# Where 76 transposes of a hybrid encoder layer are made: TensorE with an identity, or DMA transposes of two 16-bit planes

## The chip, the cores and the metric

One Trainium2 chip, one of its cores. The metric is the device time of one execution in microseconds. Lower is better. The kernel before has a median of 1718.32 us over 3 runs (1717.17 to 1718.71).

## The reference

One layer of a streaming encoder with 320 positions (256 of a new stream, 64 of a running stream that also sees 256 cached positions), d = 2048, 8 attention heads of 128, 8 gating groups of 128. Cut to what matters here:

```python
proj = rmsnorm(x) @ w_in                       # q, k, v, u, vs, gates
z = (q @ k.T) * 128**-0.5                      # per head
w = where(mask, exp(log_sigmoid(z) + log_rest), 0)   # stick-breaking weights
a = w @ v                                      # contraction over key positions
vs = rmsnorm(gelu(vs)); s = w_s @ vs + b_s     # gating: contraction over positions
bb = gelu(u) * s
merged = g_a * (a @ w_branch_a) + g_b * (bb @ w_branch_b)
h = x + merged @ w_out
y = rmsnorm(h + (silu(gu[:ff]) * gu[ff:]) @ w_down)
```

All inputs and outputs are float32. The outputs are y, the new k and v rows and the normalised vs rows of the 64 running positions.

## The kernel before, in words

Activations lie with features on the 128 partitions and the 320 positions (T) along the free dimension. Every projection is made by `block` (line 87), 128 output features at a time: the weights come in half blocks of 8 x 128 rows (512 KB) through `weights` (line 68). SP issues the load into one of 3 `raw` buffers, ScalarE rounds it to `wh` (line 75), VectorE takes the rest `wl = raw - wh` (line 76), 4 buffers each, and TensorE makes three float32r matmuls of 320 columns for each of the 8 pieces (lines 83, 84 and 85: wh with the high and the low part of the activation, wl with the high part). One half block is 24 matmuls. After each half block `tick` (line 62) counts one up and runs the functions that `at` (line 58) has put down for that tick: all work of attention and of the spatial gate is placed between half blocks in this way. A scheduler then orders each engine's instructions by what it reckons to be ready; only what goes through `keep_in_program_order` keeps its place behind its engine's previous instruction.

Attention goes by pairs of heads. `head_out` (line 421) scales a finished q, k or v block, issues the store of k and v from GpSimd, and for v copies the 64 running positions into the tile `vo` (line 431). `attend` (line 438) puts down four steps for a pair: `att_scores` 2 ticks later (scores on TensorE, lines 342 to 345, then the chain of abs, exp, ln, scan and exp on ScalarE and VectorE, lines 349 to 374, that ends in the weights `z[0]`, `z[1]` and `wown`), `att_rows` at 4 ticks (load of the cached v rows), `att_turn` at 10 ticks, `att_out` at 14 ticks. `att_turn` (line 376) makes 14 transposes of 128 x 128 float32 on TensorE against `ident`: 4 of v (line 383), 1 of `vo` (384), 6 of the prompt's weights (387), 2 of the weights on the cache (389) and 1 of `wown` (390), into 4 PSUM banks, and evacuates them with three ScalarE copies (393, 396, 397) and two VectorE copies (394, 395) to `wt` and `av`. `att_out` (line 399) multiplies from these and splits the result into the activations `aT`. A pair comes every 12 ticks; there are 4.

The spatial gate goes by pairs of groups, 4 of them: `sgu_gain` (line 477) scales vs and stores the running rows, `sgu_turn` (487) makes 5 transposes (lines 490, 491) and evacuates them with two ScalarE copies (494, 495), `sgu_mix` (499) multiplies by the masked spatial weights (503, 505) and makes `bT`. `sgu_both` (518) runs the mix of one pair and the turn of the next in one tick, every 4 ticks of the 16 that the u blocks take.

Of the kernel before, what the change touches and what calls it, by code (L numbers as in the profile page):

```python
# [8 lines left out]
F32 = mybir.dt.float32  # L9
# [4 lines left out]
P = 128  # L14
TP = 256
TS = 64
T = TP + TS
D = 2048
KD = D // P
H = 8  # L20
# [13 lines left out]
def stream_step(ctx: ExitStack, tc: tile.TileContext, xT, w_in, w_a, w_b, w_out, w_gu, w_down,  # L34
                gains, ws_t, bs, ck_t, cv, y_t, k_t, v_t, sv_t):
    nc = tc.nc
# [65 lines left out]
    def pair(name):  # L102
        return big.tile([P, 2 * T], F32, tag="D", bufs=8, name=name)
# [36 lines left out]
    ident = const.tile([P, P], F32, name="ident")  # L140
# [142 lines left out]
    attn = {}  # L283
    att_ctx = ExitStack()
    apool = att_ctx.enter_context(tc.tile_pool(name="attn", bufs=1))
# [21 lines left out]
    Z, KT = 384, T + PAST  # L307
# [13 lines left out]
    def att_new(p):  # L321
        attn[p] = {"q": apool.tile([P, 2, T], F32, tag="q", bufs=2, name="q"),
                   "k": apool.tile([P, 2, KT], F32, tag="k", bufs=2, name="k"),
                   "v": apool.tile([P, 2, T], F32, tag="v", bufs=2, name="v"),
                   "vo": apool.tile([P, P], F32, tag="vo", name="vo")}

    def att_keys(p):
        tc.keep_in_program_order(nc.sync.dma_start(
# [44 lines left out]
        for r in ROWS:  # L373
            nc.scalar.activation(out=wown[r, r], in_=z[1][r, Z:], func=AF.Exp)

    def att_turn(p):

        s = attn[p]
        z, v = s["z"], s["v"]
        ba, bb, bs_, bv = aux(), aux(), aux(), aux()  # L380
        cols = lambda t, i: t[:, i * P : (i + 1) * P]
        for i in range(4):
            nc.tensor.transpose(cols(bv, i), v[:, i // 2, i % 2 * P : (i % 2 + 1) * P], ident)  # L383
        nc.tensor.transpose(cols(ba, 3), s["vo"], ident)
        for j, b in enumerate((ba, bb)):
            for i in range(3):
                nc.tensor.transpose(cols(b, i), cols(z[j], i), ident)  # L387
        for i in range(2):
            nc.tensor.transpose(cols(bs_, i), cols(z[0], 3 + i), ident)
        nc.tensor.transpose(cols(bs_, 2), wown, ident)  # L390
        wt = s["wt"] = apool.tile([P, 3 * Z], F32, tag="wt", name="wt")
        av = s["av"] = apool.tile([P, 5 * P], F32, tag="av", name="av")
        nc.scalar.copy(out=av[:, 0 : 4 * P], in_=bv)
        nc.vector.tensor_copy(wt[:, 0:Z], ba[:, 0:Z])
        nc.vector.tensor_copy(av[:, 4 * P :], ba[:, Z:])
        nc.scalar.copy(out=wt[:, Z : 2 * Z], in_=bb[:, 0:Z])
        nc.scalar.copy(out=wt[:, 2 * Z :], in_=bs_[:, 0:Z])

    def att_out(p):
        s = attn.pop(p)  # L400
        wt, av, cvt = s["wt"], s["av"], s["cv"]
        po = aux1(), aux()
        mm = lambda out, a, b, first, last: nc.tensor.matmul(out, a, b, start=first, stop=last, skip_group_check=True)  # L403

        mm(po[0][:, TP : TP + P], av[:, 4 * P :], wt[:, 2 * Z + 2 * P :], True, False)
        for j, r in enumerate(ROWS):
            for i in range(2):
                lo = 2 * Z + i * P + j * TS
                mm(po[0][:, TP + j * TS : TP + (j + 1) * TS], cvt[:, i, j, :], wt[:, lo : lo + TS], False, i == 1)
        for j in range(2):  # L410
            mm(po[j][:, 0:TP], av[:, 2 * j * P : (2 * j + 1) * P], wt[:, j * Z : j * Z + TP], True, False)
            mm(po[j][:, P:TP], av[:, (2 * j + 1) * P : (2 * j + 2) * P], wt[:, j * Z + TP : (j + 1) * Z], False, True)
# [8 lines left out]
    def head_out(name, ps, h):  # L421
        s = attn[h // 2]
        o = s[name][:, h % 2, 0:T]
        if name == "q":
            nc.vector.scalar_tensor_tensor(out=o, in0=ps, scalar=QSCALE, in1=got["rx"],
                                           op0=ALU.mult, op1=ALU.mult)
        else:
            nc.vector.tensor_tensor(out=o, in0=ps, in1=got["rx"], op=ALU.mult)
            nc.gpsimd.dma_start(out=(k_t if name == "k" else v_t)[h], in_=o)
        if name == "v":  # L430
            nc.gpsimd.tensor_copy(s["vo"][:, ROWS[h % 2]], o[:, TP:T])

    def first_out():
        for name, b in (("q", 0), ("k", 1), ("v", 2)):
# [33 lines left out]

    us, _ = halves(H, "us")
    bT: dict[int, tuple] = {}  # L470
    vown, vnat = {}, {}

    def sgu_norm():
        got["rv"] = rms("rv", [sq.total], H * P)
        sgu_gain(0)

    def sgu_gain(p):

        own = vown[p] = apool.tile([P, 2, T], F32, tag="q", bufs=2, name="vown")[:, 0, 0:P]
        for j in range(2):  # L480
            g = 2 * p + j
            for out, r in ((vs[g][:, 0:TP], slice(0, TP)), (own[:, j * TS : (j + 1) * TS], slice(TP, T))):
                nc.vector.scalar_tensor_tensor(out=out, in0=vs[g][:, r], scalar=g_sgu[:, g : g + 1],
                                               in1=got["rv"][:, r], op0=ALU.mult, op1=ALU.mult)
            nc.gpsimd.dma_start(out=sv_t[g], in_=own[:, j * TS : (j + 1) * TS])

    def sgu_turn(p):
        pt, po = aux(), aux()
        for i in range(4):
            nc.tensor.transpose(pt[:, i * P : (i + 1) * P], vs[2 * p + i // 2][:, i % 2 * P : (i % 2 + 1) * P], ident)  # L490
        nc.tensor.transpose(po[:, 0:P], vown.pop(p), ident)
        t = apool.tile([P, 5 * P], F32, tag="av", name="vsn") if p % 2 else apool.tile([P, 3 * Z], F32, tag="wt", name="vsn")
        vn = vnat[p] = t[:, 0 : 5 * P].rearrange("p (i d) -> p i d", i=5)
        nc.scalar.copy(out=vn[:, 0:4].rearrange("p i d -> p (i d)"), in_=pt)
        nc.scalar.copy(out=vn[:, 4], in_=po[:, 0:P])
        if p + 1 < H // 2:
            sgu_gain(p + 1)
# [20 lines left out]
    def sgu_both(p):  # L518
        if p:
            sgu_mix(p - 1)  # L520
        if p < H // 2:
            sgu_turn(p)
# [14 lines left out]
    for m in range(KD):  # L537
        gate = []
        for i in range(2):
            ps = block(w_in[5 * H + i * KD + m], xs)  # L540
            t = t320("ev")
# [8 lines left out]
        t = t320("mg", 1)  # L550
# [5 lines left out]
        lo = mpool.tile([P, T], F32R, tag="C", bufs=32, name="ml")  # L556
# [72 lines left out]
    ms, r = (const.tile([P, 3], F32, name=f"col{i}") for i in range(2))  # L629
# [9 lines left out]
    for n in (1, 1, 2, 2, 2, 2, 2, 2, 1, 1):  # L639
        y = ypair[done // 2].rearrange("p (c t) -> p c t", c=2)[:, done % 2 : done % 2 + n, :]  # L640
# [57 lines left out]
```

## Time and profile before

| | |
|---|---|
| median of 3 runs | 1718.32 us |
| profiled execution, its time | 1716.78 us |
| its span, first to last instruction | 1715.0 us |
| mean granted TensorE clock | 0.998 |
| attention of the first pair to the last gate mix | about 60 to 327 us of the span |
| VectorE, ScalarE, GpSimd busy over the span | 861.9, 658.8, 46.1 us |
| DMA engines' mean rate | 154 GB/s |

The profiled execution is 1.78 us longer than its span (what lies outside the first and the last instruction), and 1.54 us below the median. In the profile's rows, PE is TensorE's matmul, DVE VectorE, ACT ScalarE, POOL GpSimd, SPq the queue of SP that issues loads. A timeline row gives start, duration, engine, line, operation, output and inputs, how many were merged, and in brackets the idle time before it with what ended it. A row of waits gives total, number of times and longest, in us. A row of DMA issues ends with the KB of one and the median us from issue to landing. A row of groups ends with busy us, mean ns of one, and the engine's idle time before.

### The profile page before, as it was taken

The numbers are of one execution on the slowest core, as the hardware profiler recorded it, in microseconds if no ns is written. First come the engines' busy times: TensorE is split into PE (matmuls) and PEld (weight loads), VectorE is DVE, ScalarE is ACT, GpSimd is POOL, SyncE is SP. The second block draws the span as 40 slices with busy tenths as digits, with TensorE's granted clock in tenths as the row PEclk, the third lists the DMA queues.
The fourth block names the chain that finished last, engine by engine and source line by source line (L and its number), as shares of the span: only waits on it lengthen the run. The fifth ranks groups of instructions, "written<-read, shape, count | busy, mean of one in ns | idle before, by whom it ended". The sixth has DMA issues, their size and how long they took to land.

```text
span 1715.0 us, 27450 instructions
## 1 busy us (share of the span) xinstructions
PE 1702.2 (99%) x11616; PEld 1696.7 (99%) x11616; DVE 861.9 (50%) x1097; ACT 658.8 (38%) x819; POOL 46.1 (3%) x73
## 2 busy tenths in 40 slices
PE   9999999999999999999999999999999999999997
PEld 9999999999999999999999999999999999999997
DVE  7655446544444445555444444444444444444454
ACT  6454454433333333444333332233333323333332
POOL 0100011000000000110000000000000000000000
PEclk9999999999999999999999999999999999999999
DMA  7554444444444445554444445444444444444453
GB/s 260 162 193 143 144 154 145 139 148 148 149 153 152 148 152 165 174 171 149 150 148 148 150 152 153 148 148 148 152 151 152 148 148 150 151 153 149 130 150 114
DMA packets 80331, 263.32 MB, mean 154 GB/s; under 512 B 9008, under 2 KB 15408, under 8 KB 80208
## 3 DMA queue, kind: packets, MB, share of 16 engines
q1 hardware_dynamic: 78704, 258.25, 46.6%
q0 software_dynamic: 1088, 3.02, 0.5%
q8 instruction: 91, 1.49, 0.3%
q10 hardware_dynamic: 416, 0.31, 0.1%
q14 instruction: 32, 0.26, 0.0%
HBM read 256.03 MB, written 5.51 MB: 152 GB/s over the span
## 4 chain that ended last, share of the span: by engine, by line
issue 54%; PE 45%; DVE 0%; DMA 0%; ACT 0%; POOL 0%; POOLq 0%; ACTq 0%; DVEq 0%
PE acc L83 13%; PE acc L84 13%; PE acc L85 13%; PE aux L219 2%; PE acc L219 1%; PE aux L403 1%; DVE h L637 0%; DMA raw<-w_in 0%; PE aux L505 0%; PE aux L343 0%; PE aux L345 0%; PE aux L387 0%; PE aux L342 0%; PE aux L490 0%; PE aux L383 0%
## 5 line engine op out<-in xcount | busy, mean ns | idle before, releaser
L75 ACT CAST wh<-raw 128x1024 fp32r<-128x1024 f32 x468 | 484.5, 1036 | 988.0 <-PE acc L84 796.3
L76 DVE TENSOR_TENSOR wl<-raw,wh 128x1024 fp32r<-128x1024 f32 x468 | 564.2, 1206 | 506.4 <-ACT wh L75 503.9
L83 PE MATMUL acc<-A,wh 128*128 128x320 f32 x2464 | 763.1, 310 | 0.0
L85 PE MATMUL acc<-A,wl 128*128 128x320 f32 x2464 | 761.5, 309 | 0.0
L84 PE MATMUL acc<-A,wh 128*128 128x320 f32 x2464 | 761.4, 309 | 0.0
L83 PEld LDWEIGHTS acc<-A,wh 128*128 128x128 f32 x2464 | 462.6, 188 | 2.1 <-issue 2.0
L84 PEld LDWEIGHTS acc<-A,wh 128*128 128x128 f32 x2464 | 462.6, 188 | 0.2
L85 PEld LDWEIGHTS acc<-A,wl 128*128 128x128 f32 x2464 | 462.6, 188 | 0.0
L85 PE MATMUL acc<-B,wl 128*128 128x320 f32 x960 | 296.6, 309 | 0.0
L83 PE MATMUL acc<-B,wh 128*128 128x320 f32 x960 | 296.6, 309 | 0.0
L84 PE MATMUL acc<-B,wh 128*128 128x320 f32 x960 | 296.6, 309 | 0.0
L83 PEld LDWEIGHTS acc<-B,wh 128*128 128x128 f32 x960 | 180.2, 188 | 0.0
L84 PEld LDWEIGHTS acc<-B,wh 128*128 128x128 f32 x960 | 180.2, 188 | 0.0
L85 PEld LDWEIGHTS acc<-B,wl 128*128 128x128 f32 x960 | 180.2, 188 | 0.0
L83 PE MATMUL acc<-mh,wh 128*128 128x320 f32 x256 | 79.1, 309 | 0.0
L84 PE MATMUL acc<-ml,wh 128*128 128x320 f32 x256 | 79.1, 309 | 0.0
L85 PE MATMUL acc<-mh,wl 128*128 128x320 f32 x256 | 79.1, 309 | 0.0
L597 DVE TENSOR_TENSOR bb<-acc,rh 128x320 f32<-128x320 f32 x44 | 21.6, 491 | 57.8 <-PE acc L85 57.8
L594 DVE TENSOR_TENSOR ev<-acc,rh 128x320 f32<-128x320 f32 x44 | 21.6, 491 | 56.4 <-PE acc L85 56.3
L83 PEld LDWEIGHTS acc<-mh,wh 128*128 128x128 f32 x256 | 48.0, 188 | 0.0
L84 PEld LDWEIGHTS acc<-ml,wh 128*128 128x128 f32 x256 | 48.0, 188 | 0.0
L85 PEld LDWEIGHTS acc<-mh,wl 128*128 128x128 f32 x256 | 48.0, 188 | 0.0
(173 smaller groups left out, 696.2 us busy)
## 6 DMA issues: line engine op xcount, KB each, us to landing
raw<-w_gu SPq DMA_DIRECT2D x176, 512.0 KB, 3.5
raw<-w_in SPq DMA_DIRECT2D x141, 512.0 KB, 3.6
raw<-w_down SPq DMA_DIRECT2D x80, 512.0 KB, 3.5
raw<-w_out SPq DMA_DIRECT2D x32, 512.0 KB, 3.6
raw<-w_a SPq DMA_DIRECT2D x16, 512.0 KB, 3.5
raw<-w_b SPq DMA_DIRECT2D x16, 512.0 KB, 3.5
raw<-w_down SPq DMA_DIRECT2D x16, 256.0 KB, 2.7
xr<-xT SPq DMA_DIRECT2D x16, 160.0 KB, 2.6
```

Source lines behind the costliest of these rows:

```text
L75: nc.scalar.copy(out=wh[:, : n * P], in_=raw[:, : n * P])
L76: nc.vector.tensor_tensor(out=wl[:, : n * P], in0=raw[:, : n * P], in1=wh[:, : n * P].bitcast(F32), op=ALU.subtract)
L83: nc.tensor.matmul(ps[:, :T], a, x[0], start=first, stop=False)
L84: nc.tensor.matmul(ps[:, :T], a, x[1], start=False, stop=False)
L85: nc.tensor.matmul(ps[:, :T], b, x[0], start=False, stop=last)
L219: nc.tensor.matmul(first[b][h][:, :T], w[:, (h * n + j) * P : (h * n + j + 1) * P], xs[c + j][i], start=not last and c + j + i == 0, stop= ...
L403: mm = lambda out, a, b, first, last: nc.tensor.matmul(out, a, b, start=first, stop=last, skip_group_check=True)
L594: nc.vector.tensor_tensor(out=t, in0=pg, in1=got["rh"], op=ALU.mult)
L597: nc.vector.tensor_tensor(out=u, in0=pu, in1=got["rh"], op=ALU.mult)
```

## The change

The 76 transposes leave TensorE. In their place GpSimd splits the float32 source into two planes of 16 bits that stand one after the other in a tile (`apart`), SP issues one DMA transpose of 8 or 10 blocks of 128 x 128 16-bit values for the whole tile (`turn`), and VectorE copies the turned planes back into the float32 layout (`together`). One pair of heads has three such tiles: v with its running rows (`vp`, 10 blocks), the weights of `z[0]` (`wp0`, 10) and those of `z[1]` with `wown` (`wp1`, 8). One pair of gating groups has one (`vsp`, 10). That makes 16 DMA transposes, 16 VectorE copies and 40 GpSimd copies. The PSUM evacuations of the transposes go, and so do the `vo` copies.

```diff
+    def planes(name, n):
+        return pair(name)[:, 0:n].bitcast(U16).rearrange("p (w n) -> p n w", w=2)
+    def apart(to, src):
+        nc.gpsimd.tensor_copy(to, src.bitcast(U16).rearrange("p (n w) -> p n w", w=2))
+    def turn(src):
+        n = src.shape[1]
+        to = planes("turned", n)
+        flat = lambda t: t.rearrange("p n w -> p w n").rearrange("p w n -> p (w n)")
+        tc.keep_in_program_order(nc.sync.dma_start(
+            out=flat(to).rearrange("p (b r) -> p b r", r=P), in_=flat(src), transpose=True))
+        return to
+    def together(to, src):
+        nc.vector.tensor_copy(to.bitcast(U16).rearrange("p (n w) -> p w n", w=2), src.rearrange("p n w -> p w n"))
...
+        y = s["wp"] = planes("wp0", 5 * P), planes("wp1", 4 * P)
+        apart(y[0], z[0])
+        apart(y[1][:, 0:Z], z[1][:, 0:Z])
+        apart(y[1][:, Z:], wown)
...
-        for i in range(4):
-            nc.tensor.transpose(cols(bv, i), v[:, i // 2, i % 2 * P : (i % 2 + 1) * P], ident)
...
-        nc.vector.tensor_copy(wt[:, 0:Z], ba[:, 0:Z])
+        s[what] = [turn(t) for t in ((s["vp"],) if what == "vt" else s["wp"])]
+    def att_join(p, what):
...
+            together(av, t[0])
...
+            together(wt[:, 0 : 5 * P], t[0])
+            together(wt[:, 5 * P :], t[1])
...
         at(now + 2, att_scores, p)
-        at(now + 4, att_rows, p)
-        at(now + 10, att_turn, p)
-        at(now + 14, att_out, p)
+        at(now + 6, att_turn, p, "vt")
+        at(now + 8, att_rows, p)
+        at(now + 8, att_join, p, "vt")
+        at(now + 12, att_turn, p, "wt")
+        at(now + 14, att_join, p, "wt")
+        at(now + 16, att_out, p)
...
-    for p in range(H // 2 + 1):
-        at(base + 4 * p + 2 + (p == 0), sgu_both, p)
+    for p, mix in enumerate((9, 11, 14, 18)):
+        at(base + 1 + 3 * p, sgu_gain, p)
+        at(base + 6 + 3 * p, sgu_turn, p)
+        at(base + (8, 10, 13, 16)[p], sgu_join, p)
+        at(base + mix, sgu_mix, p)
```

The order of instructions moves as follows. On TensorE, in the middle of the half blocks behind the first pair's scores (wh and wl are a half block's weights, A an activation, `aux` a PSUM bank), before:

```order
L85 MATMUL acc_997<-A_496,wl_1032 128x320
L383 MATMUL aux_1062<-ident_79,v_623 128x128 x4
L384 MATMUL aux_1059<-ident_79,vo_624 128x128
L387 MATMUL aux_1059<-ident_79,z0_775 128x128 x3
L387 MATMUL aux_1060<-ident_79,z1_776 128x128 x3
L389 MATMUL aux_1061<-ident_79,z0_775 128x128 x2
L390 MATMUL aux_1061<-ident_79,wown_617 128x128
L83 MATMUL acc_1091<-A_154,wh_1094 128x320
```

and at the same place of the changed kernel:

```order
L85 MATMUL acc_1009<-A_496,wl_1044 128x320
L83 MATMUL acc_1078<-A_154,wh_1081 128x320
L84 MATMUL acc_1078<-A_155,wh_1081 128x320
L85 MATMUL acc_1078<-A_154,wl_1082 128x320
L83 MATMUL acc_1078<-A_162,wh_1081 128x320
```

The 14 transposes are gone and one half block follows the other. In the queue of SP, from the cached keys of the second pair on (`raw` is a half block of weights), before:

```order
L328 DMA k<-ck_t 128x2x256
L70 DMA raw<-w_in 128x1024 [waits DMAHW3_49,DVE_49]
L70 DMA raw<-w_in 128x1024 [waits DMAHW4_49,DMAHW0_49,DVE_49]
L70 DMA raw<-w_in 128x1024 [waits DMAHW5_49,DVE_49]
L292 DMA wst<-ws_t 128x1024
L70 DMA raw<-w_in 128x1024 [waits DMAHW7_49,DVE_49]
```

and now:

```order
L348 DMA k<-ck_t 128x2x256
L70 DMA raw<-w_in 128x1024 [waits DMAHW2_49,DVE_49]
L70 DMA raw<-w_in 128x1024 [waits DMAHW3_49,DVE_49]
L340 DMA_TRANSPOSE turned<-vp 128x10x128 [waits Pool_49]
L70 DMA raw<-w_in 128x1024 [waits DMAHW5_49,DVE_49]
L340 DMA_TRANSPOSE turned<-wp_806 128x10x128 [waits Pool_49]
L340 DMA_TRANSPOSE turned<-wp_807 128x8x128 [waits DMAHW4_49,Activation_49,Pool_49]
L292 DMA wst<-ws_t 128x1024
L70 DMA raw<-w_in 128x1024 [waits DMAHW7_49,DMAHW6_49,DVE_49]
```

Three DMA transposes now stand between loads of weights, and each waits for GpSimd. On VectorE, behind the last step of the first pair's score chain (line 370 before, 390 now), before:

```order
L370 TENSOR_TENSOR z_775<-z_775,e 128x640
L76 TENSOR_TENSOR wl<-raw,wh 128x1024 x3
L428 TENSOR_TENSOR k<-acc,rx 128x320
L76 TENSOR_TENSOR wl<-raw,wh 128x1024 x2
L425 SCALAR_TENSOR_TENSOR q<-acc,rx 128x320
L76 TENSOR_TENSOR wl<-raw,wh 128x1024 x2
L428 TENSOR_TENSOR v<-acc,rx 128x320
L76 TENSOR_TENSOR wl<-raw,wh 128x1024
L394 COPY wt<-aux 128x384
L395 COPY av<-aux 128x128
```

and now:

```order
L390 TENSOR_TENSOR z_776<-z_776,e 128x640
L76 TENSOR_TENSOR wl<-raw,wh 128x1024 x3
L448 TENSOR_TENSOR k<-acc,rx 128x320
L76 TENSOR_TENSOR wl<-raw,wh 128x1024
L345 COPY av<-turned 128x2x640
L76 TENSOR_TENSOR wl<-raw,wh 128x1024
L345 COPY wt<-turned 128x2x640
L445 SCALAR_TENSOR_TENSOR q<-acc,rx 128x320
L76 TENSOR_TENSOR wl<-raw,wh 128x1024
L345 COPY wt<-turned 128x2x512
L76 TENSOR_TENSOR wl<-raw,wh 128x1024
L448 TENSOR_TENSOR v<-acc,rx 128x320
```

The joins (line 345) stand four to seven half blocks behind the score chain, each between two splits of weights.

More of the change, by code (lines that the diff above doesn't have):

```diff
@@ L374, in att_scores, with att_turn @@
             nc.scalar.activation(out=wown[r, r], in_=z[1][r, Z:], func=AF.Exp)
-    def att_turn(p):
-        s = attn[p]
-        z, v = s["z"], s["v"]
-        ba, bb, bs_, bv = aux(), aux(), aux(), aux()
-        cols = lambda t, i: t[:, i * P : (i + 1) * P]
-        for i in range(4):
[L383 to L397, printed above, removed]
+        y = s["wp"] = planes("wp0", 5 * P), planes("wp1", 4 * P)
+        apart(y[0], z[0])
+        apart(y[1][:, 0:Z], z[1][:, 0:Z])
+        apart(y[1][:, Z:], wown)
+    def att_turn(p, what):
+        s = attn[p]
+        s[what] = [turn(t) for t in ((s["vp"],) if what == "vt" else s["wp"])]
+    def att_join(p, what):
+        s = attn[p]
+        t = s[what]
+        if what == "vt":
+            av = s["av"] = apool.tile([P, 5 * P], F32, tag="av", name="av")
+            together(av, t[0])
+        else:
+            wt = s["wt"] = apool.tile([P, 9 * P], F32, tag="wt", name="wt")
+            together(wt[:, 0 : 5 * P], t[0])
+            together(wt[:, 5 * P :], t[1])
     def att_out(p):
@@ L403, in att_out @@
         mm = lambda out, a, b, first, last: nc.tensor.matmul(out, a, b, start=first, stop=last, skip_group_check=True)
[L405 removed]
+        mm(po[0][:, TP : TP + P], av[:, 4 * P :], wt[:, 8 * P :], True, False)
         for j, r in enumerate(ROWS):
             for i in range(2):
[L408 removed]
+                lo = Z + i * P + j * TS
                 mm(po[0][:, TP + j * TS : TP + (j + 1) * TS], cvt[:, i, j, :], wt[:, lo : lo + TS], False, i == 1)
         for j in range(2):
[L411 to L412 removed]
+            w = wt[:, j * 5 * P : j * 5 * P + Z]
+            mm(po[j][:, 0:TP], av[:, 2 * j * P : (2 * j + 1) * P], w[:, 0:TP], True, False)
+            mm(po[j][:, P:TP], av[:, (2 * j + 1) * P : (2 * j + 2) * P], w[:, TP:], False, True)
         aT[2 * p] = split("B", po[0][:, 0:T])
@@ L430, in head_out @@
         if name == "v":
-            nc.gpsimd.tensor_copy(s["vo"][:, ROWS[h % 2]], o[:, TP:T])
+            j = h % 2
+            if j == 0:
+                s["vp"] = planes("vp", 5 * P)
+            apart(s["vp"][:, j * TP : (j + 1) * TP], o[:, 0:TP])
+            apart(s["vp"][:, 4 * P + j * TS : 4 * P + (j + 1) * TS], o[:, TP:T])
     def first_out():
@@ L470, in stream_step @@
     bT: dict[int, tuple] = {}
-    vown, vnat = {}, {}
+    vplane, vturned, vnat = {}, {}, {}
     def sgu_norm():
         got["rv"] = rms("rv", [sq.total], H * P)
-        sgu_gain(0)
     def sgu_gain(p):
-        own = vown[p] = apool.tile([P, 2, T], F32, tag="q", bufs=2, name="vown")[:, 0, 0:P]
+        own = apool.tile([P, 2, T], F32, tag="q", bufs=2, name="vown")[:, 0, 0:P]
         for j in range(2):
@@ L485, in sgu_gain, with sgu_join @@
             nc.gpsimd.dma_start(out=sv_t[g], in_=own[:, j * TS : (j + 1) * TS])
+        y = vplane[p] = planes("vsp", 5 * P)
+        for j in range(2):
+            apart(y[:, j * TP : (j + 1) * TP], vs[2 * p + j][:, 0:TP])
+        apart(y[:, 4 * P :], own)
     def sgu_turn(p):
[L488 to L497, printed above, removed]
+        vturned[p] = turn(vplane.pop(p))
+    def sgu_join(p):
+        t = apool.tile([P, 5 * P], F32, tag="av", name="vsn") if p % 2 else apool.tile([P, 9 * P], F32, tag="wt", name="vsn")
+        together(t[:, 0 : 5 * P], vturned.pop(p))
+        vnat[p] = t[:, 0 : 5 * P].rearrange("p (i d) -> p i d", i=5)
     def sgu_mix(p):
```

9 lines of the change are left out of this document (2 added, 7 removed).

## The prediction, made before the changed kernel ran

> **What bounds the kernel now.** I read the page's busy times first, then who waited for whom, TensorE's waits apart.
>
> ```profile
> PE 1702.2 (99%) x11616; PEld 1696.7 (99%) x11616; DVE 861.9 (50%) x1097; ACT 658.8 (38%) x819; POOL 46.1 (3%) x73
> ```
> ```profile
> PE aux L190 <- POOL ones L143: 1.2, 1, 1.2
> PE acc L219 <- ACT wh L209: 1.0, 1, 1.0
> PE aux L635 <- POOL col L631: 0.2, 1, 0.2
> ```
> ```profile
> ACT wh L75 <- PE acc L84: 796.3, 360, 3.5
> SPq L70 <- DVE wl L76: 1404.5, 464, 13.8
> ```
>
> TensorE is busy for 99% of the span, and that alone would say little. But its three waits are 2.4 us in all, and none lies in the stage that changes. The others wait for it instead: ScalarE 796.3 us for a free `wh`, SP 1404.5 us for a free `raw`. So TensorE's issue sets the end, and whatever leaves it shortens the run one for one, as long as the weights stay ahead of it.
>
> **What goes: 76 transposes.** Their price is not their duration but what they push the next matmul back by.
>
> ```profile
> 93.03 0.31 PE L85 MATMUL acc<-A,wl 128*128 128x320 f32 x1
> 93.18 0.60 PE L383 MATMUL aux<-ident,v 128*128 128x128 f32 x4
> 93.61 0.27 PE L384 MATMUL aux<-ident,vo 128*128 128x128 f32 x1
> 93.72 0.82 PE L387 MATMUL aux<-ident,z 128*128 128x128 f32 x6
> 94.38 0.38 PE L389 MATMUL aux<-ident,z 128*128 128x128 f32 x2
> 94.59 0.27 PE L390 MATMUL aux<-ident,wown 128*128 128x128 f32 x1
> 94.62 0.39 PE L83 MATMUL acc<-A,wh 128*128 128x320 f32 x1
> 94.85 0.31 PE L84 MATMUL acc<-A,wh 128*128 128x320 f32 x1
> ```
>
> A matmul of 320 columns starts every 0.147 us (93.03 to 93.18). With the group, two steps take 94.85 - 93.03 = 1.82 us, without it 0.29: 1.53 us for 14 transposes, 0.109 us each. Four pairs of heads: 6.12 us. For the gate I compare a mix with transposes behind it with the last mix, which has none.
>
> ```profile
> 278.41 0.31 PE L85 MATMUL acc<-A,wl 128*128 128x320 f32 x1
> ...
> 279.67 0.60 PE L490 MATMUL aux<-ident,vs 128*128 128x128 f32 x4
> 280.11 0.27 PE L491 MATMUL aux<-ident,vown 128*128 128x128 f32 x1
> 280.13 0.39 PE L83 MATMUL acc<-A,wh 128*128 128x320 f32 x1
> ...
> 325.64 0.31 PE L85 MATMUL acc<-A,wl 128*128 128x320 f32 x1
> ...
> 326.82 0.39 PE L83 MATMUL acc<-A,wh 128*128 128x320 f32 x1
> ```
>
> 1.72 against 1.18 us: 0.54 us for 5, again 0.109 each. Four: 2.2 us. **Together 8.3 us** leave TensorE. All other matmuls stay, in number and shape.
>
> The duration of one such row is longer, 0.27 us, since rows overlap. [...]
>
> **What VectorE gets.** Its copies of this kind show a price per column.
>
> ```profile
> L394 DVE COPY wt<-aux 128x384 f32<-128x384 f32 x4 | 2.2, 550 | 0.0
> L395 DVE COPY av<-aux 128x128 f32<-128x128 f32 x4 | 1.1, 280 | 0.0
> ```
>
> (550 - 280) / 256 = 1.05 ns a value and 0.15 us fixed. A join of 1280 values of 16 bits is then 1.49 us, one of 1024 1.22 us; at best, if 16-bit values in SBUF go at twice the rate, half of that. A pair of heads adds 4.2 us and loses the two copies (0.83): 3.4 us net. A pair of groups adds 1.5. In all 19 us.
>
> ```profile
> 160.00:250.00 90.00, 90.00 (x623) 88.90 (x622) 49.50 (x71) 47.88 (x70) 9.14 (x11) 1.00 0.45 146
> ```
>
> In this stretch of the attention stage VectorE is busy 49.5 of 90 us. A pair comes every 12 half blocks, some 47 us with its own matmuls, of which about 21 are idle: the work fits, and ScalarE loses five copies. I cost it at nothing. What could cost is the place.
>
> **Where the cover is thin.** The split that follows a score chain is barely in time.
>
> ```profile
> 77.90 3.49 DVE L76 TENSOR_TENSOR wl<-raw,wh 128x1024 fp32r<-128x1024 f32 x3
> ...
> 84.00 1.23 DVE L76 TENSOR_TENSOR wl<-raw,wh 128x1024 fp32r<-128x1024 f32 x1 [2.21 <-ACT wh L75]
> ...
> 88.72 1.22 DVE L76 TENSOR_TENSOR wl<-raw,wh 128x1024 fp32r<-128x1024 f32 x1
> ```
> ```profile
> 79.39 0.31 PE L85 MATMUL acc<-A,wl 128*128 128x320 f32 x1
> ```
>
> The first of the three splits ends at 79.1 and is read at 79.39: 0.3 us of lead. A half block takes TensorE 24 x 0.147 = 3.52 us, so the fourth split (ends 85.2) is read at 89.95, 4.7 us of lead; the sixth (ends 89.9) at 98.5, 8.6 us. The joins stand behind the fourth, fifth and sixth split in the new order, so nothing of the change lies ahead of the thin one, and the lead grows from there. The 1.53 us that TensorE gains come off the leads behind it.
>
> **What waits, and for what.** SP's transposes wait for GpSimd, and behind them stand loads of weights, for these ScalarE, then VectorE, then TensorE. VectorE's joins wait for the landing, behind them splits and the drains of `acc`. GpSimd's splits wait for ScalarE's last exp, behind them the stores of k and v.
>
> ```profile
> 79.14 2.60 SPq L70 DMA_DIRECT2D raw<-w_in  x3
> ...
> 85.25 3.50 SPq L70 DMA_DIRECT2D raw<-w_in  x2
> ```
> ```profile
> 79.20 0.73 ACT L371 ACTIVATE z<-z 128x640 f32<-128x640 f32 x1
> ```
> ```profile
> 103.83 0.41 PE L83 MATMUL acc<-A,wh 128*128 128x320 f32 x1
> ```
> ```profile
> raw<-w_in SPq DMA_DIRECT2D x141, 512.0 KB, 3.6
> cv<-cv SPq DMA_DIRECT2D x4, 256.0 KB, 3.0
> sv_t<-vown POOLq DMA_DIRECT2D x8, 32.0 KB, 2.0
> ```
>
> For the first pair: `z[0]` is ready at 79.9. The transposes of the weights stand ahead of the load that SP issues at 85.3 now (seventh of the splits), whose matmuls begin at 103.83, after the change at 102.3. That load needs 3.6 us to land, 1.0 for the cast and 1.2 for the split; with the join of 1.2 ahead of that split it must be issued by **95**.
>
> GpSimd's copy of 16-bit pairs shows nowhere. The nearest rows:
>
> ```profile
> L289 POOL MEMSET wso<- 128x512 f32 x1 | 0.5, 527 | 36.5 <-DVE wl L210 36.5
> L175 POOL TENSOR_TENSOR sq_v<-sq_v,sq 128x320 f32<-128x320 f32 x7 | 7.3, 1046 | 58.2 <-ACT sq L174 58.2
> ```
> ```profile
> 55.90 0.25 POOL L431 COPY vo<-v 128x64 f32<-128x64 f32 x1
> ...
> 94.75 1.06 POOL L431 COPY vo<-v 128x64 f32<-128x64 f32 x2
> ```
>
> A write alone is 1.0 ns a value, two reads and a write 3.3, and a short copy 0.25 / 64 = 3.9 in one place and 0.53 / 64 = 8.3 in another, its fixed part included. I take 2 (one read, one write), so `wp0` is ready at 79.9 + 2.6 = 82.5 and `wp1` at 84.5; both ends stay for the range.
>
> A DMA transpose shows nowhere either. It moves 320 KB: by bytes it lies between the `cv` and the `raw` load, some 3.2 us to landing. By runs it is ten blocks of 128 rows of 256 bytes, each like one `sv_t` store: 10 x 2.0 = 20 us if they don't overlap. A single instruction whose rows spread over 16 DMA engines is nearest to the loads, so I take 3.2 us, less than that of it holding SP. Then the load behind both goes out at about 84.5 + 3 = 88, **7 us before it is needed**, and the joins are done before theirs. If each holds SP for t, the second is over at 84.5 + 2t at most: the slack is gone at t = 5 us. The other pairs have the same order, and the gate one transpose at a time. Cost: nothing.
>
> **Sum.** 1716.78 - 8.3 = 1708.5 for the profiled execution; the median stood 1.54 higher: **1710.0 us**. The PE rows of `L383` to `L390` and `L490` are gone in the new order and the matmuls close up, so a change that does not do what it says is excluded.
>
> **Rivals.**
>
> Slow transposes, the rival on the other side. SP and VectorE wait in their queues, so every us of t above 5 is paid twice by the couple `wp0`, `wp1` of each of 4 pairs, 8 us per us. The gain is spent at t = 6. At t = 8.5 it is 4 x 7 = 28 us: 1738. At 20 us each that couple alone costs 120 us: 1830. For it: the small runs of 256 bytes, both turned and read from SBUF, and a queue that may be busy with loads. Against it: the bytes are few, the DMA engines' share is 0.45. Chance 0.22.
>
> [...]
>
> Slow splits on GpSimd. At 8.3 ns a value `wp0` and `wp1` take 19 us and are ready at 99; the load goes out at 101, 6 us late. Four pairs: 24 - 8.3 = +16 us, 1734 with the median's offset. It decides from about 6.5 ns on. For it: the same `vo` copy took twice as long in one place as in another. Against: long instructions pay the fixed part once. Chance 0.11.
>
> Half and half: a t near 5, or 6 ns, or a join that comes late in one or two pairs eats 2 to 8 us of the gain: 1712 to 1718. Chance 0.10.
>
> **How the numbers follow.** Forecast 0.57, alone 1708 to 1712. Rivals 0.22, 0.11, 0.10. Below 1708 there is nothing to gain: 8.3 us is all that TensorE loses, and three runs lay within 1.5 us. Up to 1738 the range takes in the half case, GpSimd's and the milder half of the slow transposes; beyond lies about 0.12, and 0.03 below. A measurement of this kernel tells about 0.2%, 3.4 us, from no change. Faster by more: 0.57 and part of the half case, 0.61. Within: 0.07. Slower: 0.32.
>
> **What would show it.** Right: no PE waits between 60 and 330 us, the PE span shorter by 8 us, the splits' lead behind the joins still over 2 us, a DMA transpose landing in 3 to 5 us, GpSimd's split of 640 pairs under 4 us. Wrong: waits `PE acc L85 <- DVE wl L76` in that stretch. If these go back to joins that wait for a landing, or to casts that wait for `raw`, the transposes were slow; if SP waits long for `POOL wp0`, the splits were. Wrong too would be a slower `wl` split (1206 ns now) beside GpSimd's copies.

## The result and the profile after

The changed kernel takes **1724.39 us** (median of 6, 1720.67 to 1728.37), the kernel before beside it 1717.8 us: ratio 1.0038, 95% interval 1.0028 to 1.0048. It is slower by 0.38%, where 1710.0 us, faster by 0.45%, was forecast. The profiled execution took 1720.67 us (span 1718.9 us): 3.9 us above the profiled one of before, 12.2 us above the 1708.5 us of the sum. It is the shortest of the six executions, so the traces show the change at its best.

What TensorE should lose, it lost. In the stage that changed it waits for one thing alone (first line; the second is its weight loads). From the waits of the changed kernel (total us, times, longest):

```profile
PE acc L85 <- DVE wl L76: 8.9, 10, 2.1
PEld acc L85 <- DVE wl L76: 12.2, 12, 2.3
ACT wh L75 <- DMA raw<-w_in: 68.6, 28, 11.3
SPq L340 <- POOL wp L334: 17.3, 5, 4.6
```

That is the first of the signs that the prediction named for "wrong". Its two causes there, late transposes and late splits on GpSimd, both leave some trace here: ScalarE waits 68.6 us for `raw` where it was 17.9, and SP 17.3 us for the planes. But the third sign, a slower `wl` split, named in the last sentence of the prediction, is the largest. The engines' busy times between 48 and 330 us, before and after:

```profile
48.00:330.00 282.00, 282.00 (x1947) 277.89 (x1946) 159.54 (x252) 137.17 (x190) 24.85 (x40) 1.00 0.47 154
```
```profile
48.00:330.00 282.00, 272.95 (x1842) 265.76 (x1841) 215.78 (x252) 123.81 (x165) 128.17 (x72) 1.00 0.60 168
```

The columns are TensorE, its weight loads, VectorE, ScalarE, GpSimd, clock, DMA share. TensorE had no idle time and now has 9 of the 12.2 us (matmuls beside a wait also show longer, 0.41 against 0.31 us); GpSimd got 103 us more, and **VectorE 56 us** more with the same 252 instructions in the stretch, where the prediction gave it 19. The groups of VectorE in that stretch, before and after:

```profile
L76 DVE TENSOR_TENSOR wl<-raw,wh 128x1024 fp32r<-128x1024 f32 x71 | 86.4, 1222 | 68.3 <-ACT wh L75 68.3
L483 DVE SCALAR_TENSOR_TENSOR vs<-vs,gain,rv 128x256 f32<-128x256 f32 x8 | 3.7, 479 | 0.0
```
```profile
L76 DVE TENSOR_TENSOR wl<-raw,wh 128x1024 fp32r<-128x1024 f32 x70 | 117.0, 1681 | 29.0 <-ACT wh L75 28.4 <-PE acc L84 0.6
L345 DVE COPY av<-turned 128x1280 uint16<-128x1280 uint16 x4 | 11.6, 2910 | 0.0
L509 DVE SCALAR_TENSOR_TENSOR vs<-vs,gain,rv 128x256 f32<-128x256 f32 x8 | 9.9, 1232 | 0.0
...
L345 DVE COPY vsn<-turned 128x1280 uint16<-128x1280 uint16 x4 | 3.9, 984 | 8.2 <-DMA turned<-vsp 8.2
```

The same split of weights takes 1681 ns in the mean instead of 1222 (70 x 0.459 = 32 us), the same gain of `vs` 1232 instead of 479. Two joins of one shape, `av` and `vsn`, take 2910 and 984 ns. So the price of a VectorE instruction now depends on when it runs. The timeline of VectorE and of GpSimd at one place (start, us, xcount; the third pair):

```profile
169.65 1.22 DVE L76 TENSOR_TENSOR wl<-raw,wh 128x1024 fp32r<-128x1024 f32 x1
170.78 0.22 DVE L437 TENSOR_TENSOR B<-aux,B 128x64 fp32r<-128x64 f32 x1
170.91 10.28 DVE L76 TENSOR_TENSOR wl<-raw,wh 128x1024 fp32r<-128x1024 f32 x2
```
```profile
170.16 10.62 POOL L334 COPY wp<-z 128x1280 uint16<-128x1280 uint16 x2 [13.39 <-issue]
180.34 2.08 POOL L334 COPY wp<-wown 128x256 uint16<-128x256 uint16 x1
```
```profile
177.26 0.41 PE L85 MATMUL acc<-A,wl 128*128 128x320 f32 x1 [0.83 <-DVE wl L76]
181.25 0.42 PE L85 MATMUL acc<-A,wl 128*128 128x320 f32 x1 [0.21 <-DVE wl L76]
```

Two splits of 1.22 us take 10.28 us, about as long as the two copies that GpSimd runs beside them, and at the end of each TensorE stands. And the copies are dear themselves:

```profile
L334 POOL COPY wp<-z 128x1280 uint16<-128x1280 uint16 x4 | 28.9, 7223 | 45.6 <-issue 28.6 <-ACT z L391 17.0
```

7.2 us for 1280 values of 16 bits, 5.6 ns each; 2 ns was taken. All 40 copies are some 120 us, 6.2 ns for each of 19456 values, the fixed part of the short ones included.

**Theory** from these rows: GpSimd's copies and VectorE's instructions keep each other from running, and VectorE's late splits of weights stall TensorE ("contention"). **Rivals:** the copies only last long, SP waits for their planes, and loads of weights stand behind it ("late planes", a rival of the prediction); the DMA transposes hold SP ("slow transposes", another); or the joins' own time on VectorE.

### The profile page after: what moved, and what is told of

Read it like the earlier page. It is cut to its first block, busy times and chain, and to the rows that moved or that the text cites. A ratio compares the mean times of both kernels' runs of the same rounds, so it can differ in the third digit from the quotient of the medians.

```text
span 1718.9 us, 27353 instructions
## 1 busy us (share of the span) xinstructions
PE 1697.1 (99%) x11540; PEld 1688.5 (98%) x11540; DVE 921.6 (54%) x1105; ACT 648.7 (38%) x798; POOL 149.4 (9%) x105
## 4 chain that ended last, share of the span: by engine, by line
issue 57%; PE 32%; DVE 5%; DMA 3%; ACT 1%; POOL 1%; SPq 0%; POOLq 0%; DVEq 0%; ACTq 0%
PE acc L85 10%; PE acc L83 10%; PE acc L84 10%; DVE wl L76 3%; DMA raw<-w_in 2%; PE aux L219 2%; PE acc L219 1%; DVE e L387 1%; POOL wp L334 0%; DMA turned<-vsp 0%; DVE h L660 0%; ACT wh L75 0%; DMA turned<-wp 0%; DVE e L380 0%; DVE av L345 0%
## 5 line engine op out<-in xcount | busy, mean ns | idle before, releaser
L76 DVE TENSOR_TENSOR wl<-raw,wh 128x1024 fp32r<-128x1024 f32 x468 | 595.9, 1275 | 466.6 <-ACT wh L75 465.9
L85 PEld LDWEIGHTS acc<-A,wl 128*128 128x128 f32 x2464 | 462.4, 188 | 12.2 <-DVE wl L76 12.2
L175 POOL TENSOR_TENSOR sq_h<-sq_h,sq 128x320 f32<-128x320 f32 x15 | 16.4, 1095 | 457.5 <-ACT sq L174 457.5
L334 POOL COPY wp<-z 128x1280 uint16<-128x1280 uint16 (+1 forms) x8 | 44.9, 5826 | 45.6 <-issue 28.6
```

The source lines that it names most:

```text
L76: nc.vector.tensor_tensor(out=wl[:, : n * P], in0=raw[:, : n * P], in1=wh[:, : n * P].bitcast(F32), op=ALU.subtract)
L85: nc.tensor.matmul(ps[:, :T], b, x[0], start=False, stop=last)
L175: (engine or nc.gpsimd).tensor_tensor(out=self.total, in0=self.total, in1=sq, op=ALU.add)
L334: nc.gpsimd.tensor_copy(to, src.bitcast(U16).rearrange("p (n w) -> p n w", w=2))
```

## Experiments

Each ratio is to the kernel before, run beside it on the same chip (medians 1717.5 to 1719.1 us). One more run, m1, adds copies to the kernel before only to measure how long each takes, and stands further down.

| run | what is in it | median us | ratio (95% interval) |
|---|---|---|---|
| the change | | 1724.39 | 1.0038 (1.0028 to 1.0048) |
| e1_copies_only | before + GpSimd's copies | 1721.32 | 1.0015 (1.0007 to 1.0024) |
| e2_turns_only | before + DMA transposes | 1719.28 | 1.0003 (0.9994 to 1.0012) |
| e3_split_on_scalar | change, copies on ScalarE | 1743.08 | 1.0144 (1.0131 to 1.0158) |
| e4_turn_weights_later | change, weights turned later | 1736.75 | 1.0095 (1.0078 to 1.0112) |
| c0_no_split | change without the copies | 1710.10 | 0.9957 (0.9944 to 0.9971) |
| c1_split_unread | change, nobody waits for the copies | 1723.20 | 1.0030 (1.0018 to 1.0041) |
| c2_writes_alone | c1 with memsets for copies | 1710.48 | 0.9956 (0.9943 to 0.9968) |
| f1_pool_by_plane | change, copies in plane order | 1710.28 | 0.9955 (0.9943 to 0.9967) |
| f2_split_on_vector | the same on VectorE | 1709.73 | 0.9952 (0.9940 to 0.9965) |
| f3_scalar_by_plane | the same on ScalarE | 1710.39 | 0.9954 (0.9942 to 0.9967) |
| f4_vector_by_value | on VectorE in value order | 1719.52 | 1.0008 (0.9999 to 1.0017) |
| h1_copies_and_turns | e1 + DMA transposes | 1728.38 | 1.0061 (1.0049 to 1.0074) |
| h2_copies_and_joins | e1 + joins | 1739.59 | 1.0126 (1.0111 to 1.0142) |
| h3_copies_turns_joins | e1 + both | 1738.85 | 1.0124 (1.0110 to 1.0138) |

### Parts of the change put into the kernel before

e1 adds these lines behind the exps, and the like for `vp` and `vsp`:

```
+        y = planes("wp0", 5 * P), planes("wp1", 4 * P)
+        apart(y[0], z[0])
+        apart(y[1][:, 0:Z], z[1][:, 0:Z])
+        apart(y[1][:, Z:], wown)
...
```

> The kernel before with GpSimd's 40 copies into two planes added and nothing else: TensorE still transposes, no DMA transposes, no joins, and nothing reads the planes (added work; the outputs stay). Contention theory (GpSimd's copies and VectorE slow each other while both run, and the late `wl` splits stall TensorE): the `wl` split between 48 and 330 us goes from 1222 to 1450-1700 ns, VectorE's busy time there grows by 20 us or more, TensorE waits for `wl`, and the time is 1720-1727. Late planes theory (the copies only take long; SP waits for them and the loads of weights stand behind): nobody waits for the planes here, so 1717.8 within 1.5. Slow transposes: 1717.8 too.

e2 adds only transposes, in `attend` and, one for each pair of groups, in `sgu_turn`:

```
+        at(now + 6, lambda: turn(attn[p]["v"].rearrange("p h t -> p (h t)")))
         at(now + 10, att_turn, p)
+        at(now + 12, lambda: [turn(t) for t in attn[p]["z"]])
```

> The kernel before with 16 DMA transposes added on SP at the places of the change, fed with the unsplit bits of `v`, `z` and `vs`, into tiles that nobody reads (10, 10, 7 and 10 blocks; added work, the outputs stay). GpSimd and VectorE get nothing. Slow transposes theory: the loads behind them come late and the time rises by 6 us or more, to 1724 or above. Contention and late planes theories: they wait for nothing slow, 1717.8 within 1.5, each holding SP for 1 to 3 us.

With the copies alone the splits between 48 and 330 us are as slow as in the change; with the transposes alone they are as before:

```profile
L76 DVE TENSOR_TENSOR wl<-raw,wh 128x1024 fp32r<-128x1024 f32 x71 | 123.9, 1752 | 38.4 <-ACT wh L75 38.4
```
```profile
L76 DVE TENSOR_TENSOR wl<-raw,wh 128x1024 fp32r<-128x1024 f32 x71 | 86.5, 1222 | 71.7 <-ACT wh L75 71.5
```

Contention is there as expected, but it costs only 0.15%, some 2.6 us, the low end of what was expected. TensorE's wait for `wl` in that run is short, so the leads of the kernel before seem to absorb the rest:

```profile
PE acc L85 <- DVE wl L76: 0.4, 1, 0.4
```

The transposes cost nothing that the measurement tells, though in that run the single one held SP for as long as 5.0 us and landed after 4.8 to 10.3 us. Slow transposes are out as the cause by themselves.

### The split on ScalarE, and the turn one half block later

```
     def apart(to, src):
-        nc.gpsimd.tensor_copy(to, src.bitcast(U16).rearrange("p (n w) -> p n w", w=2))
+        nc.scalar.copy(to, src.bitcast(U16).rearrange("p (n w) -> p n w", w=2))
```

> The changed kernel with the split into planes on ScalarE in GpSimd's place; everything else stays. Contention and late planes theories both: 12 us of stalls go, VectorE's `wl` split between 48 and 330 us is back at about 1220 ns, a join takes 0.75-0.9 us, SP's wait for the planes is under 3 us, and the time is 1709-1713. Slow transposes or the joins' own time: it stays at 1720 or above. By my forecast's own terms (price of a copy on ScalarE 0.73 us for 640 values, so 1.4 us for 1280) ScalarE gets some 30 us, hidden.

```
-        at(now + 12, att_turn, p, "wt")
-        at(now + 14, att_join, p, "wt")
+        at(now + 13, att_turn, p, "wt")
+        at(now + 15, att_join, p, "wt")
```

> The changed kernel with the transposes of the weights and their joins one half block later (3.5 us); GpSimd's copies stay as they are. Late planes theory: SP's wait for `wp` (17.3 us in 5 waits) shrinks to under 6, the loads get ahead, and most of the loss comes back: 1712-1718. Contention theory: VectorE is as slow as before, its `wl` splits stall TensorE at the same places, 1721-1727. Slow transposes: no change, 1724.

Both missed, and both by what they showed. On ScalarE the split is no cheaper than on GpSimd, 4 to 6 us where an exp of the same tile took 0.73. First line: its copies (ns, min/median/max); second: VectorE's joins in the same run.

```profile
L334 ACT COPY wp<-z x8: 3992/5024/6082, 81.3 to 231.8; 128x1280 uint16<-128x1280 uint16 x4, 128x768 uint16<-128x768 uint16 x4
L345 DVE COPY av<-turned x4: 893/901/914, 96.9 to 232.6; 128x1280 uint16<-128x1280 uint16 x4
```
```profile
81.32 9.59 ACT L334 COPY wp<-z 128x1280 uint16<-128x1280 uint16 x2
...
91.55 3.31 ACT L334 COPY vp<-v 128x512 uint16<-128x512 uint16 x2
94.37 3.23 ACT L75 CAST wh<-raw 128x1024 fp32r<-128x1024 f32 x3
```
```profile
95.76 0.63 PE L83 MATMUL acc<-A,wh 128*128 128x320 f32 x1 [4.59 <-ACT wh L75]
```

The joins are all near 0.9 us without GpSimd's copies beside them, as the contention theory says. But ScalarE's casts of weights stand behind 13 us of copies (81.32 to 94.37), and TensorE waits for `wh`. So the copy is slow for a reason of its own, on two engines.

In e4 the transposes of the first pair's weights did not come 3.5 us later. SP had six loads ahead of them, which waited for free `raw` buffers:

```profile
97.32 21.86 SPq L70 DMA_DIRECT2D raw<-w_in  x6
119.24 1.56 SPq L340 DMA_TRANSPOSE turned<-wp  x1
```
```profile
133.35 0.79 PE L422 MATMUL aux<-wt,av 128*128 128x128 f32 x2 [10.83 <-DVE wt L345]
```

They came at 119.24 instead of 87.39, and the matmuls that read `wt` waited 10.8 us. This run tells the late planes theory nothing, since it replaced one wait by a longer one.

### Contention and lateness told apart

```
+    zero = apool.tile([P, 5 * P], F32, name="zero")
...
-            out=flat(to).rearrange("p (b r) -> p b r", r=P), in_=flat(src), transpose=True))
+            out=flat(to).rearrange("p (b r) -> p b r", r=P), in_=zero[:, 0:n].bitcast(U16), transpose=True))
```

c1 is this; in c0 the calls of `apart` are left out too.

> The changed kernel without GpSimd's copies (left out), its DMA transposes fed from a tile of zeros, so that attention and gate come out as zeros; the transposes, VectorE's joins and all matmuls stay. Contention and late planes theories: nothing of the 12 us is left, 1709.5 within 1.5, the forecast's sum. If the transposes' hold on SP or the joins' own time on VectorE cost something, it shows here: 1713 or more.

> As the one before, but GpSimd's 40 copies run as in the changed kernel, with nobody waiting for their planes: the transposes read the tile of zeros (so the split's result is left out of the outputs), SP's order is the changed kernel's. Late planes theory: with no wait for planes the 12 us are gone, 1709-1712. Contention theory: VectorE is as slow beside the copies as in the changed kernel (joins up to 3-4 us, `wl` splits between 48 and 330 us about 1650 ns) and at least half of the stalls stay: 1716-1724. This run less the one before is what contention alone costs, the changed kernel less this one what the late planes cost.

c0 takes 1710.10 us, the forecast was 1710.0: transposes, joins and their places cost nothing. c1, where the transposes read no plane and SP waits for GpSimd's copies 0.9 us in all instead of 17.3, gives 1.0030. **The copies' mere presence costs 0.73%, 13 us**; that their planes come late adds 0.08%, 1.4 us, which the two intervals don't tell from nothing. Part of the 13 us is a lower clock, some 3 us by an estimate from c1's trace (last section). c0, then c1, the same stretch, and TensorE's wait in c1:

```profile
L76 DVE TENSOR_TENSOR wl<-raw,wh 128x1024 fp32r<-128x1024 f32 x74 | 89.8, 1219 | 45.9 <-ACT wh L75 45.7
...
L347 DVE COPY av<-turned 128x1280 uint16<-128x1280 uint16 x4 | 3.6, 904 | 5.5 <-DMA turned<-zero 5.5
```
```profile
L76 DVE TENSOR_TENSOR wl<-raw,wh 128x1024 fp32r<-128x1024 f32 x69 | 113.8, 1660 | 26.1 <-ACT wh L75 26.1
L347 DVE COPY av<-turned 128x1280 uint16<-128x1280 uint16 x4 | 11.7, 2917 | 0.0
```
```profile
PE acc L85 <- DVE wl L76: 8.5, 7, 3.4
```

Late planes, the rival as the prediction priced it, falls.

### Reading or writing

```
     def apart(to, src):
-        nc.gpsimd.tensor_copy(to, src.bitcast(U16).rearrange("p (n w) -> p n w", w=2))
+        nc.gpsimd.memset(to, 0)
```

> As c1_split_unread (1723.2), with each of GpSimd's 40 copies turned into a memset of the same planes with the same jumping writes: GpSimd writes and reads nothing (the split is left out; attention and gate come out as zeros). Exclusive use theory by reading: a split of weights reads two tiles, GpSimd's memset none, so `wl` takes 1206 ns beside it and the time is 1710-1713; the joins may still be held. Shared bandwidth theory (any GpSimd traffic of that length slows VectorE): `wl` splits up to 3-6 us as in c1, 1718-1724. [...]

GpSimd is at work nearly as long for a tile of 1280 values, 5.98 us against 7.26 in c1, and VectorE's splits don't feel it:

```profile
L336 POOL MEMSET wp<- 128x1280 uint16 x4 | 23.9, 5980 | 0.1
```
```profile
L76 DVE TENSOR_TENSOR wl<-raw,wh 128x1024 fp32r<-128x1024 f32 x74 | 89.9, 1221 | 40.3 <-ACT wh L75 40.1
L347 DVE COPY vsn<-turned 128x1280 uint16<-128x1280 uint16 x4 | 10.7, 2672 | 8.9 <-DMA turned<-zero 8.9
```

1.0030 becomes 0.9956. A split reads two tiles of SBUF (`raw`, `wh`). In the mean of the stage it takes 1221 ns where GpSimd only writes and 1660 where it reads and writes; in c1, 25 splits lie beside a copy for over half of their time, and the longest takes 6.3 us. In the changed kernel's trace such a split ends with the copy beside it: the `wp` copies of the third pair end at 176.76 and 180.77 and the splits beside them at 177.20 and 181.19, those of the fourth pair at 224.90 and 228.89 and the splits at 225.30 and 229.28, 0.4 us behind each copy. The joins, which read one tile, can be held by the writes too: in c2 the third pair's `av` join starts at 166.74 beside a memset that ends at 167.69 and takes 1.72 us, and the `vsn` joins take 2672 ns in the mean (904 in c0 for both). So it is not GpSimd's traffic as such: copies that read and write held the splits, memsets that only write did not, and a join was held by either. Why splits and joins differ in this, no run shows. One reservation: the memsets wait for no data, so they start earlier than the copies, but by the trace 13 splits still ran beside one for over nine tenths of their time, and none took over 1.23 us.

The memset also gives the price of the writes alone, with no split held: 5.98 us, 4.7 ns a value, for writes that jump between two planes. The memset of 512 numbers in the kernel before, which writes straight, took 1.0 ns a value.

### The order of the copy

```
     def apart(to, src):
-        nc.gpsimd.tensor_copy(to, src.bitcast(U16).rearrange("p (n w) -> p n w", w=2))
+        nc.gpsimd.tensor_copy(to.rearrange("p n w -> p w n"), src.bitcast(U16).rearrange("p (n w) -> p w n", w=2))
```

The same values go to the same places, low halves first, then high ones. f1 is this on GpSimd; f2 on VectorE, f3 on ScalarE; f4 is the change's own order on VectorE.

> The kernel before with copies of 128x640 numbers added in the last stages, read by nobody (added work): on GpSimd in value order (reads straight, writes jump between two planes), in plane order (reads every second 16-bit value, writes straight), flat as 16 bits and flat as f32; on ScalarE and VectorE in value and plane order. If the jumping order is what makes the split slow, plane order is at most half (under 3.5 us on GpSimd against 6 to 7); if it is the 16-bit type, flat 16 bits is as slow as the split and f32 half of that or less. Contention theory: `wl` splits beside a GpSimd copy are longer than 1206 ns, beside every kind that reads and writes SBUF.

> The changed kernel with the same 40 copies on GpSimd, but plane after plane (reads every second 16-bit value, writes straight) where the change goes value after value (writes jump between the planes). Exclusive use theory (a GpSimd copy and a VectorE instruction that reads two tiles of SBUF don't run together, whichever came second waits to the other's end): a copy of 1280 values takes 1.5-2.2 us alone against 5.8, so GpSimd's copies take some 35 us and not 115, VectorE is held for 10 us and not 44, and most of the loss goes: 1710-1714. If any GpSimd copy beside the splits is enough, whatever its length: 1718 or more.

> The changed kernel with the split on VectorE, plane after plane as its joins go, in GpSimd's place. Contention and late planes theories: no GpSimd copies beside VectorE, and planes in time if VectorE splits at the price of its joins (0.75 ns a value, 1.0 us for 1280): its busy time grows by 15 us against the change without copies, `wl` splits at 1220 ns, SP's wait for the planes under 3 us: 1709-1714, the rest being splits of weights that stand behind these copies where the lead was 0.3 us. Slow transposes or joins: 1720 or more.

> The split on ScalarE as in e3_split_on_scalar (1743), but plane after plane. If the order of the writes is what made it slow there (6.2 against 1.56 us for 1280 values in m1_prices), ScalarE gets some 35 us and not 98, its casts are late by 2-3 us at most after a score chain, and the time is 1710-1714. If 16 bits on ScalarE or its place in the queue ahead of the casts is to blame, 1725 or more.

> The split on VectorE as in f2_split_on_vector (1709.7), but value after value as in the change. By m1_prices (3.1 us for 1280 values against 1.1) VectorE gets some 60 us in place of 13 and the splits of weights behind come late: 1716-1726, with TensorE waiting for `wl` and no GpSimd beside. If only GpSimd's company counts, it is as fast as the other order, 1710-1712.

What 1280 values on a partition cost in m1, a single execution of 1742.45 us that is used for these durations alone (ns, min/median/max; they ran in bunches, so the least is nearest to the copy alone):

```profile
L582 POOL COPY pool_value<-src x3: 6963/8748/9870, 772.4 to 798.3; 128x1280 uint16<-128x1280 uint16 x3
L585 POOL COPY pool_plane<-src x3: 1487/2193/4942, 780.7 to 804.9; 128x1280 uint16<-128x1280 uint16 x3
L588 POOL COPY pool_flat<-src x3: 1251/1508/1837, 807.0 to 812.3; 128x1280 uint16<-128x1280 uint16 x3
L591 POOL COPY pool_f<-src x3: 717/977/1709, 808.8 to 813.8; 128x640 f32<-128x640 f32 x3
L594 ACT COPY act_value<-src x3: 5867/6195/6535, 773.3 to 791.9; 128x1280 uint16<-128x1280 uint16 x3
L597 ACT COPY act_plane<-src x3: 1477/1556/1825, 778.7 to 800.1; 128x1280 uint16<-128x1280 uint16 x3
L600 DVE COPY dve_value<-src x3: 3085/4055/9008, 772.4 to 788.2; 128x1280 uint16<-128x1280 uint16 x3
L603 DVE COPY dve_plane<-src x3: 1102/1752/6596, 786.8 to 806.0; 128x1280 uint16<-128x1280 uint16 x3
```

Value order against plane order: 4.7 times on GpSimd, 4.0 on ScalarE, 2.8 on VectorE. 16 bits alone are cheap (`pool_flat`, 1251 ns against 717 for the same bytes as 640 float32). In plane order it is the reads that step, over every second value, and they cost little (1487 against 1251 ns on GpSimd); in value order the reads are straight and the writes jump from plane to plane, and that order is dear on all three engines (6963 ns on GpSimd, 5867 on ScalarE, 3085 on VectorE). What makes it dear the rows don't show: value order also writes in runs of two values, and no run tells the jumps from the short runs.

In plane order all three kernels land within 0.7 us of each other, at the forecast: f1 0.9955, f2 0.9952, f3 0.9954. GpSimd still holds VectorE in f1, only shorter, and no TensorE wait for `wl` is left:

```profile
L334 POOL COPY wp<-z 128x1280 uint16<-128x1280 uint16 x4 | 9.6, 2402 | 49.3 <-issue 32.6 <-ACT z L391 16.6
...
L76 DVE TENSOR_TENSOR wl<-raw,wh 128x1024 fp32r<-128x1024 f32 x74 | 94.0, 1277 | 40.5 <-ACT wh L75 40.1 <-PE acc L85 0.3
```

All of GpSimd's copies are now 37.5 us, 1.9 ns a value: the 2 that the prediction took. On VectorE in plane order a copy of 1280 values is 820 ns; in value order, f4, with GpSimd free, TensorE waits for `wl` again:

```profile
L334 DVE COPY wp<-z 128x1280 uint16<-128x1280 uint16 x4 | 12.4, 3102 | 0.0
```
```profile
PE acc L85 <- DVE wl L76: 5.7, 6, 2.2
```

f4's 1.0008 is 0.56% above f2. So the order alone costs some 10 us even where GpSimd holds nobody, by VectorE's own time; these waits are 5.7 us of the 10.

### Why the copies alone cost little

Open was why the copies cost 13 us in c1 and 2.6 in e1, with the splits held as long.

```
+    def side(what, p, src):
+        for t in src:
+            to = turn(t)
+            at(state["tick"] + 2, together, pair("joined")[:, 0 : t.shape[1]], to)
```

This is h3, called for `vp`, `wp` and `vsp` at the places of the change. h1 has the transpose without the join; in h2 `to` is a tile of zeros.

> e1_copies_only with the 16 DMA transposes of the planes added at the places of the change; nobody reads what they give (added work, the outputs stay), TensorE keeps its transposes. If loads of weights behind the transposes use up the leads (ScalarE waited 17.9 us for `raw` in the kernel before, 46.7 in c0_no_split and 68 in c1_split_unread): 1724 or more, up to 1731. If it is the joins or TensorE's faster pace: as e1, ratio 1.0015, 1718-1722.

> e1_copies_only with VectorE's 16 joins added at the places of the change, from a tile of zeros into tiles that nobody reads; no DMA transposes, TensorE keeps its own (added work, the outputs stay). If the joins, held by the copies too (28 us in the changed kernel), use up the leads: 1724-1731. If it is the loads or the pace: 1719-1722.

> e1_copies_only with the transposes and the joins added: all of the change's new work, with TensorE's 76 transposes kept and used (added work, the outputs stay). If joins and transposes together use up the leads: 13 us above the kernel before, 1728-1733. If TensorE's faster pace is what makes the rest late: at most 5 us above, 1719-1723.

TensorE's faster pace is not needed for the loss: h3 has the old pace and loses 1.2%. Transposes alone cost nothing (e2), on top of the copies 0.46% (h1); the joins cost nothing without the copies (c0), on top of them 1.1% (h2). In each TensorE waits longest for `wl`, where e1 had 0.4 us of it; h1, then h2:

```profile
PE acc L85 <- DVE wl L76: 5.2, 3, 2.5
```
```profile
PE acc L85 <- DVE wl L76: 15.9, 5, 6.7
```

The reading that fits: holds, joins and late loads use up one and the same lead, that of the splits before TensorE; the first to come is nearly free, the second is paid. The leads themselves were not followed through these runs. The parts don't add (h3 is no more than h2), and h2 and h3 lose more than c1 does. Their long waits explain part of that (below); the scheduler's order also differs between these kernels, and the remainder was not settled.

## Why the prediction was wrong, point by point

- **76 transposes leave TensorE, 8.3 us: right.** c0, f1, f2 and f3 are below before by 0.43 to 0.48%, 7.4 to 8.2 us, with all 76 gone. The 0.109 us a row from the starts of matmuls was the right price, and the row's own duration, 0.272 us in the mean and 20.7 us for 76, was not.
- **VectorE's joins, 1.49 and 1.22 us, nothing on the path: right in c0**, where they cost 0.90 and 0.75 us, between that price and half of it, and nothing waits. In the change `av` took 2.9 us.
- **DMA transposes at 3.2 us to landing: somewhat low, harmless.** In the changed kernel (ns on SP, min/median/max, and landing):

```profile
L340 SPq DMA_TRANSPOSE turned<-wp x8: 1232/1398/2985, 87.4 to 241.6; - x8
...
DMA to landing us min/median/max: 3.0/5.1/6.5
```

  That is far from the 20 us by runs. Slow transposes, the rival with 0.22, did not happen.
- **The step that failed is the price of GpSimd's copies, "I take 2 (one read, one write)"; and what they take from VectorE stood in the sum at nothing.** The jumping writes alone are 4.7 ns a value (c2), and a copy is 6.2 in the change, its holds and fixed parts included; the prediction did not ask in which order a copy writes. While they run they hold VectorE: its splits of weights took 32 us longer in the stage, and TensorE waited for them. It takes both. f1 has the hold with copies of 2 ns and takes 1710.28, at the forecast's 1710.0; c2 has the jumping writes without the hold on the splits and takes 1710.48.
- **The rival "slow splits on GpSimd" had the price in its bounds but the wrong path.** It lets late planes delay loads and decides from 6.5 ns on. In the change the copies of a pair's weights take 12.3 to 14.2 us for 2304 values, 5.3 to 6.2 ns, so they stayed below that, and c1 shows that the loss stays when nobody waits for the planes. The path was through VectorE: "the work fits" counted its 21 idle us in 47 and nothing that GpSimd takes from it. The slower `wl` split stood in the last sentence as a sign, without price or chance; it is the cause.
- **"The lead grows from there": false beside copies.** The copies of `wp` start just behind the score chain, where the lead is 0.3 us, and lie beside the splits that were to rebuild it (170.91).

## What to carry to other kernels

Ask of each copy in which order it writes: written plane after plane, the change is worth some 0.45% on any of three engines; written value after value, with the same bytes, it loses 0.38% on GpSimd and 1.44% on ScalarE, and gains nothing on VectorE. A free GpSimd is no free place for copies when VectorE's splits feed the engine that bounds: price what it holds VectorE for (32 us of splits here), beside its own time. Slack that hides one addition is gone for the next (copies alone cost 0.15%, joins without them nothing, both 1.26%), so test additions together and not only one by one.

## What else the runs showed of the chip

Behind a wait of 4.6 us TensorE came back at a granted clock of 0.50. In e3 that wait ends at 95.76, and the windows behind it, with the granted clock third from the end, show

```profile
96.00:100.00 4.00, 3.64 (x13) 3.24 (x14) 4.00 (x6) 1.59 (x2) 0.63 (x1) 0.50 0.58 200
102.00:106.00 4.00, 4.00 (x30) 4.00 (x29) 2.55 (x3) 3.06 (x3) 0.54 (x1) 1.00 0.83 312
```

with matmuls 0.267 us apart instead of 0.147 (13 starts in 4 us, where 27 would fit). h2 shows the same behind a wait of 6.7 us: 0.50 from 135 to 139. Four us at 0.50 cost some 2 us beside the wait itself, and part of what e3, h2 and h3 lose is that (mean clocks of 0.992, 0.994 and 0.993 in their profiled executions, 0.998 before).

What decides it, these runs leave open. In c1 the clock is at 0.50 from 142 to 144 and from 302 to 305, behind waits of 2.1 us (to 141.55) and of 3.4 us (to 300.81); in h1 two waits of 2.5 us are followed by nothing of the kind. In the profiled execution of the change no wait for `wl` is longer than 2.3 us, and the clock is 1.00 in the whole stretch. But that execution has a mean clock of 0.998, and the longest of the six, 1728.37 us, one of 0.995. By an estimate from these two, a lower clock makes 0.003 of 1728 us, some 5 of the 7.7 us between them; no trace shows where.
